# Dense products of a hybrid diffusion layer: three fp32r products of split operands, or one fp32 product

## The chip, the core and the metric

The kernel runs on one core of a Trainium2 chip. The metric is device microseconds of one execution. Five engines with queues of their own share the work: TensorE (PE: matmuls, with the weight loads shown apart as PEld), VectorE (DVE), ScalarE (ACT), GpSimd (POOL) and SyncE (SP), which issues nearly all of the DMAs here.

## What is computed

One layer of a bidirectional RWKV-7 mixer beside a gated short convolution, over 128 context tokens and 2048 latent tokens (2176 in all) of 1024 channels. Cut to the dense products:

```python
h = rmsnorm(x, norm_g) * (1 + scale) + shift        # (2176, 1024)
proj = h @ w_in                                      # 1024 -> 4096: r, k, v, g_a, b, c, u, g_b of 512 each
lw = tanh(h @ decay_down);  w = w0 + lw @ decay_up   # two directions, 64 wide
la = h @ iclr_down;         a = sigmoid(bias + la @ iclr_up)
kk = kk * rsqrt(max(sum(kk * kk, per head), 1e-24))  # 8 heads of 64
...                                                  # delta-rule scan, both directions; short convolution
bonus = sum(r * kd * bonus_rk, per head)
u = concat(ya * silu(g_a), yb * silu(g_b)) @ w_out   # 1024 -> 1024
y = rmsnorm(x + gate * u, final_g)
```

Everything is fp32 in memory.

## The kernel before

**Split products.** TensorE has a matmul in fp32r, a reduced form of fp32. The kernel gets nearly full precision from it in this way: an operand x is copied to fp32r (the high part, by ACT), and x minus that copy is the low part (by DVE or POOL). A product is then three fp32r matmuls that add up in PSUM: high by high, high by low, low by high (lines 182 to 184 for the input projection, 1503 to 1505 for the output projection). Where one operand is exact in fp32r (a matrix of ones), or where the contraction has only 64 rows, so that both parts of the data can be stacked on 128 partitions (lora-up), two matmuls do.

**Phase 1** (`phase1`) makes the input projection. The tokens are cut into six blocks `BLK` (five of 384, one of 256), taken in three thirds of two blocks. The 34 column blocks of 128 (`cb`: 16 for k, r, v, g of the recurrence, 16 for the convolution, 2 for lora-down) each need 8 slices of the contraction, so a column block on a token block is one call of `dense`, 8 slices. `make_h` normalises a block into h with both parts. `load_w` brings a column block of the weights: the first time the raw weights come from the input (512 KB, `raw_w`), are split (`high_w` on ACT, `low_w`), and both parts are stored to a scratch tensor `wsp` in HBM (1024 KB); in the second and third thirds they are loaded from there (1024 KB). `lora_down` makes the four operands of lora-up with high and low parts stacked. In each third `recurrence` goes through 8 units (4 channel groups by 2 blocks). The order of its work on PE, DVE, ACT and POOL is written out by hand: `UNIT_FIRST` for the first third, `UNIT` for the others, lists of words, each a few instructions, with the unit that it belongs to (`+-1`: the one before). Words that matter here: `k r v g` are projections, `w0 w1 a0 a1` lora-up, `bb` and `ss` sums over a head (matmuls with a block matrix of ones), `hs ls hb lb` the split of their operands, `xk yk` and the like the split of the next weights. Then `groupB` makes the convolution's part, four column blocks a group.

**Phase 2** is the chunked recurrence: products of 64- and 32-wide tiles in plain fp32 (psF, psG, psE, psX, psS and so on), with an inverse of small triangular matrices on POOL. Its first pieces run beside the last third of phase 1. Its order is a list too (`SEQ`, and `LATE` from its 13th stage on).

**Phase 3** is the output projection. Its words are woven into `LATE`: `CL/WL` load a slice of `w_out`, `CH/WH` and `CD/WD` split it, `AL cL aL` load a tile of 128 tokens of the mixed activations, `AH cH aH` and `AD cD aD` split that, and `AP P B` are the products, 512 columns each. 17 token tiles by 2 halves by 8 slices.

Two small plain fp32 products stand beside all this: the modulation rows (`mod_rows`, 32 columns of weight) and the gate row (line 636, a weight of 2 columns).

Of the kernel before, what the change touches and what calls it, by code (L numbers as in the profile page):

```python
# [6 lines left out]
F32 = mybir.dt.float32  # L7
F32R = mybir.dt.float32r
# [41 lines left out]
UNIT_FIRST = """  # L50
k al+-2 xg+-2 yg+-2 rh+-2 bb+-2 mx+-1 rc+-1 q0+-2 vs+-2 v1+-1 q1+-2 v2+-1 shv+-1 t1+-1 ov+-1 r1+-1 kk+-1
g+-1 xr+-1 yr+-1 tp+-1 kn+-1 k1 k2 kA+-1 r2+-1 a0 r s1+-1 s0+-1 shk e1+-1 shr+-1 xv+-1 kd+-1 gt+-1 ok pp+-1
c+-1 yv+-1 ta0 sq sg+-1 tv+-1 or+-1 b0+-1 ka+-1 hs a1 b1+-1 ls xk w1 w0 v ss ta1 e2+-1 yk hb+-1 t0 vm+-1
lb+-1
"""
UNIT = """
k v1+-1 vs+-2 lb+-2 mx+-1 rc+-1 s0+-1 v2+-1 w0 shv+-1 kA+-1 bb+-2 s1+-1 q0+-2 q1+-2 kk+-1 k1 a0 r1+-1 k2
pp+-1 r2+-1 ov+-1 c+-1 kn+-1 e1+-1 g+-1 ta0 shk gt+-1 kd+-1 ok shr+-1 v or+-1 e2+-1 ka+-1 b0+-1 sq b1+-1
sg+-1 al+-1 a1 hs hb+-1 t0 ls r tv+-1 rh+-1 ta1 w1 vm+-1 ss t1 tp
# [3 lines left out]
def phase1(K):  # L63
# [17 lines left out]
    ones = tp.tile([128, 128], F32, tag="pv", name="ones", bufs=1)  # L81
    nc.sync.dma_start(ones[:], A["cst"][:, 0:128])
    onr = cp.tile([128, 128], F32R, name="onr")
    V.tensor_copy(onr[:], ones[:])
    onf = cp.tile([128, 128], F32R, name="onf")
    V.tensor_scalar(onf[:], ones[:], 0.0, 1.0, ALU.mult, ALU.add)
# [30 lines left out]
    def load_up():  # L117

        raw = ta_.tile([128, 2, 2, 512], F32, tag="x", name="upraw", bufs=1)
        for h in range(2):  # L120
            nc.sync.dma_start(raw[h * 64:h * 64 + 64], A["wup"].rearrange("n (d p) c -> p n d c", d=2))
        parts = ca.tile([128, 8, 512], F32R, tag="upx", name="ups")
        hi, lo = [parts[:, i:i + 4].rearrange("p (n d) c -> p n d c", d=2) for i in (0, 4)]
        for n in range(2):
            P.copy(hi[:, n], raw[:, n])
            (V, G)[n].tensor_tensor(lo[:, n], raw[:, n], hi[:, n].bitcast(F32), ALU.subtract)
            for d in range(2):
                up[n, d] = (hi[:, n, d], lo[:, n, d])

    kept = set()  # L130
# [12 lines left out]
    def raw_w(cb):  # L143
        raw = wp.tile([128, 8, 128], F32, tag="wr", name=f"wr{cb}_{K.u()}", bufs=2)
        nc.sync.dma_start(raw[:], A["win"][cb])
        return raw

    def high_w(cb, raw):
        w = wp.tile([128, 2, 8, 128], F32R, tag="w", name=f"w{cb}_{K.u()}", bufs=4)
        P.copy(w[:, 0], raw[:])  # L150
        return w

    def low_w(cb, raw, w, eng):
        eng.tensor_tensor(w[:, 1], raw[:], w[:, 0].bitcast(F32), ALU.subtract)  # L154
        nc.sync.dma_start(S["wsp"][cb], w[:].bitcast(F32))
        kept.add(cb)

    def make_h(j, x):
        t0, n = BLK[j]
        xt, rt = x  # L160
        hh = (hr if j in (0, 3) else hl).tile([128, 2, 8, 384], F32R, tag="h", name=f"h{j}")
# [18 lines left out]
    def products(ps, w, hh, n, ks):  # L180
        for k in ks:
            T.matmul(ps[:, :n], w[:, 0, k], hh[:, 0, k, :n], start=k == 0, stop=False)  # L182
            T.matmul(ps[:, :n], w[:, 0, k], hh[:, 1, k, :n], start=False, stop=False)  # L183
            T.matmul(ps[:, :n], w[:, 1, k], hh[:, 0, k, :n], start=False, stop=k == 7)  # L184
# [29 lines left out]
    def parts_of(t_, n, nm, eng):  # L214

        hi = ta_.tile([128, 384], F32R, tag="hsh", name=f"hsh{nm}", bufs=1)
        lo = ta_.tile([128, 384], F32R, tag="hsl", name=f"hsl{nm}", bufs=1)
        P.copy(hi[:, :n], t_[:, :n])  # L218
        eng.tensor_tensor(lo[:, :n], t_[:, :n], hi[:, :n].bitcast(F32), ALU.subtract)  # L219
        return hi, lo  # L220

    def part_sum(o, t_, n, nm, eng=G):

        hi, lo = parts_of(t_, n, nm, eng)
        ps = pax.tile([128, 384], F32, tag="ax", name=f"ps{nm}")
        T.matmul(ps[:, :n], o[:], hi[:, :n], start=True, stop=False)
        T.matmul(ps[:, :n], o[:], lo[:, :n], start=False, stop=True)
        return ps

    def norm(j, xt, eng=G):  # L230
# [8 lines left out]
        ps = part_sum(onf, acc, n, f"q{j}", eng)  # L239
# [21 lines left out]
    for i, b in enumerate((0, 2, 1, 3)):  # L261
# [28 lines left out]
        if i == 0:  # L290
            xb[0] = norm(0, x0, V)
        if i == 1:
            h0 = make_h(0, xb[0])
            next(h0)
            xb[1] = norm(1, x1, V)
# [42 lines left out]
    def recurrence(t3, units, js, lws, pre, following):  # L338
# [14 lines left out]
        raws = {}  # L353
        asked, split = [], []

        def ask():
            while asked and (len(raws) < 2):
                x, cb = asked.pop(0)
                raws[x] = cb, raw_w(cb)

        def project(x, i):
# [6 lines left out]
            if u.last:  # L368
                g2 = u.g + 1
                cb = dict(k=4, r=0, v=8, g=12)[x] + g2 if g2 < 4 else dict(k=20, r=24, v=28, g=16)[x]  # L370
                if t3:
                    wts[x] = load_w(cb)
                else:
                    asked.append((x, cb))
                    ask()

        def weight(x, i, low):
            if i >= len(units) or not U[i].last or t3:
                return
            cb, raw = raws[x]  # L380
            if not low:
                wts[x] = high_w(cb, raw)
            else:
                low_w(cb, raw, wts[x], G if x in "rg" else V)
                del raws[x]
                ask()

        def word(w, i):
# [4 lines left out]
            if w[0] in "xy" and len(w) == 2:  # L393
                return weight(w[1], i, w[0] == "y")
# [31 lines left out]
            elif w in ("hs", "hb"):  # L426
                src = u.sq if w == "hs" else u.bs
                hi = one(u, "hsh" if w == "hs" else "hb", dt=F32R)
                P.copy(hi[:, :n], src[:, :n])  # L429
                setattr(u, w, hi)  # L430
            elif w in ("ls", "lb"):
                src, hi = (u.sq, u.hs) if w == "ls" else (u.bs, u.hb)
                lw_ = one(u, "hsl" if w == "ls" else "lb", dt=F32R)
                G.tensor_tensor(lw_[:, :n], src[:, :n], hi[:, :n].bitcast(F32), ALU.subtract)  # L434
                setattr(u, w, lw_)
            elif w in ("ss", "bb"):
                hi, lw_ = (u.hs, u.ls) if w == "ss" else (u.hb, u.lb)
                ps = u.ps[w] = pax.tile([128, 384], F32, tag="ax", name=f"ps{w}{g}_{j}")
                T.matmul(ps[:, :n], onr[:], hi[:, :n], start=True, stop=False)
                T.matmul(ps[:, :n], onr[:], lw_[:, :n], start=False, stop=True)  # L440
# [6 lines left out]
            elif w in ("w0", "w1", "a0", "a1"):  # L447
                which, d = "wa".index(w[0]), int(w[1])
                ps = u.ps[w] = pmm.tile([128, 384], F32, tag="mm", name=f"up{w}_{K.u()}")
                x = lws[j][which * 2 + d]  # L450
                for m, part in enumerate(up[which, d]):
                    T.matmul(ps[:, :n], part[:, g * 128:g * 128 + 128], x[:, :n], start=m == 0, stop=m == 1)
# [81 lines left out]
        seq = [(w.split("+")[0], int(w.split("+")[1]) if "+" in w else 0) for w in (UNIT if t3 else UNIT_FIRST).split()]  # L534
# [88 lines left out]
    def gate_rows():  # L623
        for b in range(2):
            pr = None
            for k2 in range(4):
                wt = wp.tile([128, 2, 512], F32, tag="wr", name=f"wgate{b}{k2}", bufs=2)
# [30 lines left out]
    def lora_down(j, wd, wi, pre):  # L658
        n = BLK[j][1]
        nm = j % 2  # L660
        lw = [ta_.tile([128, 384], F32R, tag=f"lw{i}_{nm}", name=f"lw{i}_{j}") for i in range(4)]
        for which, (w, fn) in enumerate(((wd, AF.Tanh), (wi, AF.Copy))):
            ps = pre[which] if pre else dense(w, hs[j], n, f"l{which}")
            f = ta_.tile([128, 384], F32, tag=("sq", "bs")[which], name=f"lf{which}_{j}", bufs=1)
            P.activation(f[:, :n], ps[:, :n], fn)
# [101 lines left out]
I@15 sv51@12 fa@10.1 Ge0@16 E110@13 Ev001@13 gh10@14 E010@13 Ev110@13 E100@13 gh00@14 Ev010@13 Gm1@16  # L767
# [881 lines left out]
```

## Time and profile before

| | |
|---|---|
| median of 3 runs | 1581.41 us (1579.3 to 1582.26) |
| the profiled execution, first to last instruction | 1578.3 us |
| mean granted TensorE clock | 0.982 |
| PE MATMUL records | 16208 |
| HBM read, written | 208.05 MB, 103.17 MB |

The page of the profile gives busy time by engine, the chain of work that ended last, and groups of instructions by line. A row of the timeline has the start in us, the duration in us, the engine, the line, the operation, the tiles (out<-in), the tile of the array (128\*128: contraction rows by output columns), the shape of the moving operand, and how many such instructions in a row were merged. In a group's row the numbers behind the bar are busy us and mean ns of one, then the idle time ahead of it. Matmul records overlap, since one starts before the last one's results are out; the distance between starts tells the rate.

### The profile page before, as it was taken

How to read it: one execution, taken by the hardware profiler on the slowest of the kernel's cores; microseconds unless marked ns; L12 is line 12 of the kernel's file. 1: busy time of each engine (PE TensorE's matmuls, PEld its weight loads, DVE VectorE, ACT ScalarE, POOL GpSimd, SP SyncE). 2: the span in 40 equal slices, each digit the busy share in tenths (PEclk: the TensorE clock that was granted, in tenths of full speed). 3: DMA queues.
4: the chain of work that ended last, by engine and by line, in shares of the span. 5: the costliest groups of instructions: out<-in, count | busy, mean ns of one | idle time of the engine just before them, and what ended most of it. 6: DMA issues, size and time to landing. Idle time of an engine off the chain costs nothing.

```text
span 1578.3 us, 39371 instructions
## 1 busy us (share of the span) xinstructions
PE 1499.9 (95%) x16208; PEld 1381.2 (88%) x16208; DVE 1139.9 (72%) x1957; ACT 772.3 (49%) x1462; POOL 573.8 (36%) x962
## 2 busy tenths in 40 slices
PE   5999999999999999999999998999999998899998
PEld 2899999999999999899998997888888886678786
DVE  5999995764999735449985428798998997746533
ACT  4566652432555213135551107887878777523222
POOL 0133330001333100013322805888788887212221
PEclk7899999999999999999999998999999999999999
DMA  9669998663878865438887537566676754646442
GB/s 371 213 174 264 269 270 332 223 223 115 225 220 217 233 226 180 145 116 233 261 218 267 194 125 178 150 188 159 194 192 179 193 163 149 180 142 188 151 143 93
DMA packets 204579, 313.78 MB, mean 199 GB/s; under 512 B 58088, under 2 KB 147560, under 8 KB 190320
## 3 DMA queue, kind: packets, MB, share of 16 engines
q1 hardware_dynamic: 168816, 311.13, 63.9%
q10 hardware_dynamic: 35584, 0.14, 1.4%
q8 instruction: 127, 2.08, 0.6%
q14 instruction: 52, 0.43, 0.1%
HBM read 208.05 MB, written 103.17 MB: 197 GB/s over the span
## 4 chain that ended last, share of the span: by engine, by line
PE 65%; DVE 14%; POOL 7%; issue 5%; DMA 5%; ACT 2%; SPq 0%; ACTq 0%; DVEq 0%; POOLq 0%
POOL zt L1094 4%; PE psu L1503 4%; PE psu L1504 4%; PE psu L1505 4%; PE psE L1189 3%; POOL ztmp L1091 3%; PE mmb L182 2%; PE mmb L184 2%; PE mmb L183 2%; PE psS L1220 2%; PE mmc L182 2%; PE mmc L184 2%; PE mmc L183 2%; PE mmu L182 2%; PE mmu L184 2%
## 5 line engine op out<-in xcount | busy, mean ns | idle before, releaser
L1094 POOL TENSOR_TENSOR zt<-zt,ztmp 128x30 f32<-128x30 f32 (+7 forms) x510 | 215.4, 422 | 39.8
L1091 POOL TENSOR_TENSOR ztmp<-ab,zt 128x60 f32<-128x60 f32 (+7 forms) x255 | 139.4, 547 | 66.7 <-DVE ab L1082 47.0
L410 POOL TENSOR_TENSOR sh<-rawl 128x384 f32<-128x384 f32 (+1 forms) x48 | 47.5, 1007 | 210.1 <-ACT rawl L401 210.1
L1220 PE MATMUL psS<-sv,E 128*64 128x64 f32 x2176 | 104.6, 229 | 12.8 <-DVE sv L1246 7.3
L1220 PEld LDWEIGHTS psS<-sv,E 128*64 128x64 f32 x2176 | 82.8, 137 | 37.9 <-issue 16.3
L1194 DVE TENSOR_TENSOR E<-psE,msk 128x512 f32<-128x512 f32 x136 | 90.6, 683 | 20.0 <-PE psE L1189 18.9
L1568 POOL TENSOR_TENSOR z<-z,x 128x512 f32<-128x512 f32 x32 | 42.7, 1337 | 147.6 <-DVE z L1562 85.7
L1175 ACT ACTIVATE stf<-psX 64x512 f32<-64x512 f32 x136 | 80.3, 590 | 13.1 <-PE psX L1171 10.7
L434 POOL TENSOR_TENSOR hsl<-sq,hsh 128x384 fp32r<-128x384 f32 (+1 forms) x24 | 34.1, 1421 | 129.9 <-ACT hsh L429 121.6
L1246 DVE TENSOR_TENSOR sv<-psS,pc 64x128 f32<-64x128 f32 x254 | 63.7, 271 | 22.4 <-PE psS L1220 21.7
L182 PE MATMUL mmg<-h,w 128*128 128x384 f32 (+1 forms) x216 | 70.8, 328 | 0.0
L183 PE MATMUL mmg<-h,w 128*128 128x384 f32 (+1 forms) x216 | 70.7, 327 | 0.0
L184 PE MATMUL mmg<-h,w 128*128 128x384 f32 (+1 forms) x216 | 70.7, 327 | 0.0
L219 POOL TENSOR_TENSOR hslq<-ssq,hshq 128x384 fp32r<-128x384 f32 (+1 forms) x4 | 4.8, 1202 | 174.2 <-ACT hshq L218 109.6
L182 PE MATMUL mmb<-h,w 128*128 128x384 f32 (+1 forms) x192 | 63.9, 333 | 4.0 <-DMA w<-scr_wsp 4.0
L182 PE MATMUL mmv<-h,w 128*128 128x384 f32 (+1 forms) x192 | 63.1, 329 | 0.9 <-DVE sg L524 0.6
L184 PE MATMUL mmc<-h,w 128*128 128x384 f32 (+1 forms) x192 | 62.8, 327 | 1.0 <-DVE w L154 1.0
L184 PE MATMUL mmb<-h,w 128*128 128x384 f32 (+1 forms) x192 | 63.7, 332 | 0.0
L183 PE MATMUL mmb<-h,w 128*128 128x384 f32 (+1 forms) x192 | 63.6, 331 | 0.0
L182 PE MATMUL mmu<-h,w 128*128 128x384 f32 (+1 forms) x192 | 63.0, 328 | 0.2
L182 PE MATMUL mmc<-h,w 128*128 128x384 f32 (+1 forms) x192 | 63.0, 328 | 0.0
L184 PE MATMUL mmu<-h,w 128*128 128x384 f32 (+1 forms) x192 | 62.9, 328 | 0.0
(312 smaller groups left out, 5019.6 us busy)
## 6 DMA issues: line engine op xcount, KB each, us to landing
w<-scr_wsp SPq DMA_DIRECT2D x68, 1024.0 KB, 5.4
scr_wsp<-w SPq DMA_DIRECT2D x34, 1024.0 KB, 6.0
rr<-scr_ops SPq DMA_DIRECT2D x32, 1024.0 KB, 6.7
scr_ops<-xs SPq DMA_DIRECT2D x160, 192.0 KB, 6.5
wr<-in_win SPq DMA_DIRECT2D x34, 512.0 KB, 8.2
x<-in_x SPq DMA_DIRECT2D x17, 512.0 KB, 3.9
wadas<-in_wada SPq DMA_DIRECT2D x8, 1024.0 KB, 13.9
sv<-scr_vt SPq DMA_DIRECT2D x32, 256.0 KB, 4.0
```

Source lines behind the costliest of these rows:

```text
L182: T.matmul(ps[:, :n], w[:, 0, k], hh[:, 0, k, :n], start=k == 0, stop=False)
L183: T.matmul(ps[:, :n], w[:, 0, k], hh[:, 1, k, :n], start=False, stop=False)
L184: T.matmul(ps[:, :n], w[:, 1, k], hh[:, 0, k, :n], start=False, stop=k == 7)
L1091: G.tensor_tensor(tv, ab[:, j:j + 2, j + 2:32].unsqueeze(1).broadcast_to((128, kn, 2, n)), zt[:, :kn, j:j + 2].unsqueeze(3).broadcast_to(( ...
L1094: G.tensor_tensor(zt[:, :kn, j + 2:32], zt[:, :kn, j + 2:32], tv[:, :, r], ALU.subtract)
L1175: P.activation(g.fs[64:128, :, hd, e::2], g.ps["X"][e][hr_].rearrange("p a (b t) -> p b a t", b=2), AF.Copy, scale=-1.0)
L1194: V.tensor_tensor(g.E[n][:, k:k + 2].rearrange("p a b c -> p (a b) c"), pe[:].rearrange("p a b c -> p (a b) c"), B.msk[:, ME[g.d]].unsquee ...
L1220: T.matmul(g.sp[i // 4][r, q, hd, :], g.E[n][:, k, hd, r], g.sv[:, u, hd, :], start=True, stop=True)
L1246: V.tensor_tensor(dst, g.sp[i // 4][0:64, q], B.pc[0:64, d, 2 * p:2 * p + 2, c:c + 1].broadcast_to((64, 2, 64)), ALU.mult)
L1503: T.matmul(ps[:], mh[:, n], hi[:, cs], start=start and n == 0, stop=False)
L1504: T.matmul(ps[:], mh[:, n], lo[:, cs], start=False, stop=False)
L1505: T.matmul(ps[:], ml[:, n], hi[:, cs], start=False, stop=stop and n == 3)
```

## The change

Each dense product becomes a single matmul of unsplit fp32 operands. Every split (copy to fp32r, subtraction) goes, and with them the stores of split weights and the loads of them; weights are loaded raw each time. `h`, the weights, the lora operands and the activations of the output projection need half the room, and the freed room is given to more buffers (8 of `w`, 3 each of the activations). The lora-up operands are no longer stacked: the product contracts over the 64 rows of its direction. `UNIT` loses the words of the splits, and the first third uses it as well; `LATE` loses its split words, with the others in their old order.

```diff
-UNIT_FIRST = """
...
 UNIT = """
-k v1+-1 vs+-2 lb+-2 mx+-1 ...
+k v1+-1 vs+-2 mx+-1 rc+-1 s0+-1 v2+-1 w0 shv+-1 kA+-1 bb+-2 s1+-1 q0+-2 q1+-2 kk+-1 k1 a0 r1+-1 k2 pp+-1 r2+-1 ov+-1 c+-1 kn+-1 e1+-1 g+-1 ta0 shk gt+-1 kd+-1 ok shr+-1 v or+-1 e2+-1 ka+-1 b0+-1 sq b1+-1 sg+-1 al+-1 a1 t0 r tv+-1 rh+-1 ta1 w1 vm+-1 ss t1 tp
...
-    onr = cp.tile([128, 128], F32R, name="onr")
-    V.tensor_copy(onr[:], ones[:])
+    onr = cp.tile([128, 128], F32, name="onr")
+    nc.sync.dma_start(onr[:], A["cst"][:, 0:128])
...
+        raw = ca.tile([128, 2, 512], F32, tag="upx", name="ups")
+        nc.sync.dma_start(raw[:], A["wup"].rearrange("n p c -> p n c"))
...
+                up[n, d] = raw[d * 64:d * 64 + 64, n]
...
     def load_w(cb):
-        if cb in kept:
-            w = wp.tile([128, 2, 8, 128], F32R, tag="w", name=f"w{cb}_{K.u()}", bufs=4)
-            nc.sync.dma_start(w[:].bitcast(F32), S["wsp"][cb])
-            return w
-        raw = raw_w(cb)
-        w = high_w(cb, raw)
-        low_w(cb, raw, w, V)
+        w = wp.tile([128, 8, 128], F32, tag="w", name=f"w{cb}_{K.u()}", bufs=8)
+        nc.sync.dma_start(w[:], A["win"][cb])
         return w
...
                 V.scalar_tensor_tensor(xt[:, k, c], xt[:, k, c], gs[:, k % 4, s:s + 1], rt[:, c], ALU.mult, ALU.mult)
-                P.activation(hh[:, 0, k, c], xt[:, k, c], AF.Identity, bias=sh[:, k % 4, s:s + 1])
-                V.scalar_tensor_tensor(hh[:, 1, k, c], xt[:, k, c], sh[:, k % 4, s:s + 1], hh[:, 0, k, c].bitcast(F32), ALU.add, ALU.subtract)
+                P.activation(hh[:, k, c], xt[:, k, c], AF.Identity, bias=sh[:, k % 4, s:s + 1])
...
-            T.matmul(ps[:, :n], w[:, 0, k], hh[:, 0, k, :n], start=k == 0, stop=False)
-            T.matmul(ps[:, :n], w[:, 0, k], hh[:, 1, k, :n], start=False, stop=False)
-            T.matmul(ps[:, :n], w[:, 1, k], hh[:, 0, k, :n], start=False, stop=k == 7)
+            T.matmul(ps[:, :n], w[:, k], hh[:, k, :n], start=k == 0, stop=k == 7)
...
-                T.matmul(ps[:, :n], onr[:], hi[:, :n], start=True, stop=False)
-                T.matmul(ps[:, :n], onr[:], lw_[:, :n], start=False, stop=True)
+                T.matmul(ps[:, :n], onr[:], src[:, :n], start=True, stop=True)
...
-                x = lws[j][which * 2 + d]
-                for m, part in enumerate(up[which, d]):
-                    T.matmul(ps[:, :n], part[:, g * 128:g * 128 + 128], x[:, :n], start=m == 0, stop=m == 1)
+                T.matmul(ps[:, :n], up[which, d][:, g * 128:g * 128 + 128], lws[j][which][d * 64:d * 64 + 64, :n], start=True, stop=True)
...
-            for d in range(2):
-                a, b = slice(d * 64, d * 64 + 64), slice(64 - d * 64, 128 - d * 64)
-                t_ = lw[which * 2 + d]
-                V.tensor_copy(t_[a, :n], f[a, :n])
-                V.tensor_tensor(t_[b, :n], f[a, :n], t_[a, :n].bitcast(F32), ALU.subtract)
+            P.activation(lw[which][:, :n], ps[:, :n], fn)
...
     def w_load(k):
-        raws["w", k] = O.r.tile([128, 1024], F32, tag="raw", name=f"woraw{k}", bufs=2)
-        D(raws["w", k][:], A["wout"][k * 128:(k + 1) * 128, :])
...
         if k in ATT:
+            wk[k] = K.spare((8, 4, 0, 2)[k], f"wo{k}", F32)
+        D(wk[k][:], A["wout"][k * 128:(k + 1) * 128, :])
...
+            mx = mts[a, i] = (O.r if a == "c" else O.l).tile([128, 4, 128], F32, tag=f"m{a}", name=f"m{a}{i}", bufs=3)
...
-            T.matmul(ps[:], mh[:, n], hi[:, cs], start=start and n == 0, stop=False)
-            T.matmul(ps[:], mh[:, n], lo[:, cs], start=False, stop=False)
-            T.matmul(ps[:], ml[:, n], hi[:, cs], start=False, stop=stop and n == 3)
+            T.matmul(ps[:], ms[:, n], wk[k][:, cs], start=start and n == 0, stop=stop and n == 3)
```

More of the change, by code (lines that the diff above doesn't have):

```diff
@@ L80, in phase1 @@
     nc.sync.dma_start(vec[:], A["vec"])
-    ones = tp.tile([128, 128], F32, tag="pv", name="ones", bufs=1)
-    nc.sync.dma_start(ones[:], A["cst"][:, 0:128])
-    onr = cp.tile([128, 128], F32R, name="onr")
-    V.tensor_copy(onr[:], ones[:])
-    onf = cp.tile([128, 128], F32R, name="onf")
-    V.tensor_scalar(onf[:], ones[:], 0.0, 1.0, ALU.mult, ALU.add)
+    onr = cp.tile([128, 128], F32, name="onr")
+    nc.sync.dma_start(onr[:], A["cst"][:, 0:128])
+    onf = cp.tile([128, 128], F32, name="onf")
+    V.memset(onf[:], 1.0)
     smask = ca.tile([128, 384], F32, name="smask")
@@ L160, in make_h @@
         xt, rt = x
-        hh = (hr if j in (0, 3) else hl).tile([128, 2, 8, 384], F32R, tag="h", name=f"h{j}")
+        hh = (hr if j in (0, 3) else hl).tile([128, 8, 384], F32, tag="h", name=f"h{j}")
         hs[j] = hh
@@ L212, in mod_rows, with norm @@
             T.matmul(ps[q:q + 32, :], scp[:, k, :], wt[:, i, :], start=k < 4, stop=k >= 4)
[L214 to L230, printed above, removed]
+    def norm(j, xt):
         t0, n = BLK[j]
@@ L238, in norm @@
             V.tensor_tensor(acc[:, :n], acc[:, :n], sq[:, :n], ALU.add)
-        ps = part_sum(onf, acc, n, f"q{j}", eng)
+        ps = pax.tile([128, 384], F32, tag="ax", name=f"psq{j}")
+        T.matmul(ps[:, :n], onf[:], acc[:, :n], start=True, stop=True)
         rt = ta_.tile([128, 384], F32, tag="kk", name=f"rt{j}", bufs=1)
@@ L290, in phase1 @@
         if i == 0:
-            xb[0] = norm(0, x0, V)
+            xb[0] = norm(0, x0)
         if i == 1:
@@ L294, in phase1 @@
             next(h0)
-            xb[1] = norm(1, x1, V)
+            xb[1] = norm(1, x1)
             first_products(wlora, range(4))
@@ L352, in recurrence @@
             U.append(u)
[L353 to L359, printed above, removed]
         def project(x, i):
@@ L370, in project @@
                 cb = dict(k=4, r=0, v=8, g=12)[x] + g2 if g2 < 4 else dict(k=20, r=24, v=28, g=16)[x]
[L371 to L386, printed above, removed]
+                wts[x] = load_w(cb)
         def word(w, i):
@@ L532, in word @@
                 spill("q", g, j, u.q, "q")
-        seq = [(w.split("+")[0], int(w.split("+")[1]) if "+" in w else 0) for w in (UNIT if t3 else UNIT_FIRST).split()]
+        seq = [(w.split("+")[0], int(w.split("+")[1]) if "+" in w else 0) for w in UNIT.split()]
         E = mybir.EngineType
@@ L626, in gate_rows @@
             for k2 in range(4):
[L627 removed]
+                wt = wp.tile([128, 2, 512], F32, tag="w", name=f"wgate{b}{k2}", bufs=8)
                 nc.sync.dma_start(wt[:], A["wada"][4 + b][:, k2 * 2:k2 * 2 + 2])
@@ L660, in lora_down @@
         nm = j % 2
-        lw = [ta_.tile([128, 384], F32R, tag=f"lw{i}_{nm}", name=f"lw{i}_{j}") for i in range(4)]
+        lw = [ta_.tile([128, 384], F32, tag=f"lw{i}_{nm}", name=f"lw{i}_{j}") for i in range(2)]
         for which, (w, fn) in enumerate(((wd, AF.Tanh), (wi, AF.Copy))):
             ps = pre[which] if pre else dense(w, hs[j], n, f"l{which}")
-            f = ta_.tile([128, 384], F32, tag=("sq", "bs")[which], name=f"lf{which}_{j}", bufs=1)
-            P.activation(f[:, :n], ps[:, :n], fn)
-            for d in range(2):
-                a, b = slice(d * 64, d * 64 + 64), slice(64 - d * 64, 128 - d * 64)
-                t_ = lw[which * 2 + d]
-                V.tensor_copy(t_[a, :n], f[a, :n])
-                V.tensor_tensor(t_[b, :n], f[a, :n], t_[a, :n].bitcast(F32), ALU.subtract)
+            P.activation(lw[which][:, :n], ps[:, :n], fn)
         return lw
@@ L1596, in end @@
             p.close()
[L1598 to L1600 removed]
+    K.last = dict(R=lambda _=0: begin(), Lo=lambda _=0: begin_left(), end=end, CL=w_load, WL=w_load,
+                  AL=m_load("c"), cL=m_load("c"), aL=m_load("a"), xL=x_load, ss=square_sum, rt=root, rc=inverse_root, fo=out)
     for h in range(2):
@@ L1625, in build @@
             K.S[name] = tc.dram_tile(list(shape), F32, name=f"scr_{name}")[:]
-    K.S["wsp"] = tc.dram_tile([34, 128, 2, 8, 128], F32, name="scr_wsp")[:]
     phase3(K)
```

154 lines of the change are left out of this document (41 added, 113 removed).

## The prediction, made before the change was run

> **What bounds the kernel now.** I read the page's busy shares and its chain first, then the stage table (busy time of each engine in stretches that I chose, with the number of instructions, the granted TensorE clock and the DMA share), then single records of PE.
>
> ```profile
> PE 1499.9 (95%) x16208; PEld 1381.2 (88%) x16208; DVE 1139.9 (72%) x1957; ACT 772.3 (49%) x1462; POOL 573.8 (36%) x962
> ...
> PE 65%; DVE 14%; POOL 7%; issue 5%; DMA 5%; ACT 2%; SPq 0%; ACTq 0%; DVEq 0%; POOLq 0%
> ```
>
> ```profile
> core 0: us, PE busy (x) PEld busy (x) DVE busy (x) ACT busy (x) POOL busy (x), PEclk, DMA share, GB/s
> 0.00:60.00 60.00, 39.42 (x190) 25.87 (x191) 40.91 (x99) 28.77 (x55) 2.04 (x16) 0.77 0.87 325
> 60.00:240.00 180.00, 174.63 (x998) 171.10 (x998) 170.39 (x213) 108.73 (x194) 65.11 (x49) 1.00 0.86 240
> 240.00:800.00 560.00, 559.34 (x3330) 548.27 (x3329) 387.62 (x607) 225.34 (x411) 89.38 (x77) 1.00 0.68 210
> 800.00:840.00 40.00, 35.89 (x220) 34.93 (x219) 29.93 (x52) 13.21 (x29) 6.75 (x7) 0.91 0.80 224
> 840.00:960.00 120.00, 115.42 (x1137) 111.44 (x1138) 57.77 (x116) 24.14 (x55) 42.18 (x91) 0.97 0.56 189
> 960.00:1300.00 340.00, 320.57 (x8204) 283.40 (x8202) 300.46 (x606) 267.81 (x508) 286.32 (x616) 0.99 0.65 178
> 1300.00:1371.00 71.00, 57.06 (x1214) 48.53 (x1206) 51.60 (x100) 50.37 (x86) 39.21 (x74) 0.95 0.50 151
> 1371.00:1570.00 199.00, 196.90 (x945) 157.40 (x941) 98.04 (x164) 52.93 (x128) 42.81 (x33) 1.00 0.47 152
> ```
>
> PE's busy time can't be read as work done, because records overlap (a 384-column matmul shows 0.33 us, but the next one starts 0.17 us later). What counts is the distance from start to start. The stretches that hold the dense products are 60 to 960 (input projection) and 1371 to 1570 (output projection): PE is idle there for 5.4, 0.7, 4.1, 4.6 and 2.1 us. So in nearly all of the time that the change touches, TensorE is the bound, at full clock, and whatever a product costs more or less goes into the time one to one. The middle, 960 to 1300, holds the recurrence, which the change leaves alone. DVE comes near PE in one place, 60 to 240, with 170.4 of 180 us; the change takes work away from it there.
>
> **What a dense product costs now.** In the order of time on PE, the first and the last of 24 matmuls of one block (8 slices of the contraction, three fp32r matmuls each):
>
> ```profile
> 560.67 0.34 PE L182 MATMUL mmc<-h,w 128*128 128x384 f32 x1
> ...
> 564.66 0.34 PE L184 MATMUL mmc<-h,w 128*128 128x384 f32 x1
> ```
>
> 23 steps in 3.99 us are 0.1735 us each, so one slice of 384 columns costs 3 x 0.1735 = 0.5205 us. The same reading for 256 columns (17 steps in 2.04 us) and for the 512 of the output projection (18 steps in 4.09 us):
>
> ```profile
> 940.89 0.28 PE L182 MATMUL mmgb<-h,w 128*128 128x256 f32 x1
> ...
> 942.93 0.28 PE L184 MATMUL mmgb<-h,w 128*128 128x256 f32 x1
> ```
>
> ```profile
> 1372.74 0.40 PE L1505 MATMUL psa<-woh,mlc 128*128 128x512 f32 x1
> ...
> 1376.83 0.39 PE L1505 MATMUL psa<-woh,mlc 128*128 128x512 f32 x1
> ```
>
> These give 0.120 and 0.227 us, 0.360 and 0.682 a slice.
>
> **What a plain fp32 product costs.** No plain fp32 product of full size is in the trace. The nearest is the gate row (L636): a [128 x 2] weight with 512 moving columns, amid the dense stream.
>
> ```profile
> L636 PE MATMUL psgate<-gaterow,sel x4: 590/591/592, 600.8 to 653.7; 128*2 128x512 f32 x4
> ```
>
> ```profile
> 600.54 0.34 PE L183 MATMUL mmc<-h,w 128*128 128x384 f32 x1
> 600.81 1.02 PE L636 MATMUL psgate<-gaterow,sel 128*2 128x512 f32 x2
> 601.76 0.44 PE L226 MATMUL psq<-hshq,onf 128*128 128x384 f32 x1
> ```
>
> The loop makes two such products and the trace shows four records: **an fp32 product is two matmuls on the chip**. Entering it took 0.27 us where a 384 step takes 0.1735, so a change of the tile in the array (128\*128 to 128\*2) costs 0.0965 us. Leaving it costs that again, and the rest, 0.95 - 0.0965 = 0.853 us, is two records of 0.427 us for 512 columns, 0.834 ns a column each. For 384 columns that is 0.641 us a product, for 256 0.427, for 512 0.854. The width of the weight was 2 here and will be 128; whether the wider load hides is told by the fp32 loads of 128 columns, which take 0.141 us, less than half of a 0.32 us pass:
>
> ```profile
> L1317 PEld LDWEIGHTS psT<-idt,y x68: 137/141/144, 1057.6 to 1490.6; 128*128 128x128 f32 x68
> ```
>
> Bounds: from below, two records could run side by side, as the 64-wide ones of the recurrence do (16 records of 128 columns in 1348.85 - 1347.83 - 0.0965 = 0.92 us, half of 16 x 0.107); then a 384 product costs 0.32 us. From above, four steps like today's, 4 x 0.1735 = 0.694 us.
>
> ```profile
> 1347.83 1.09 PE L1189 MATMUL psE<-stg,stf 128*64 128x128 f32 x16 [1.20 <-DVE E L1194]
> 1348.85 0.66 PE L1317 MATMUL psT<-idt,y 128*128 128x128 f32 x4
> ```
>
> I take 0.641, because the gate row is the only row with a long moving operand and no neighbour in the other columns of the array; the side-by-side rows all use two or more column halves, and a 128-wide weight has none to spare. The Trainium skill (FP8 and Floating Point Precision, TensorE Precision Notes) counts four passes for true fp32; the row agrees, 0.853 us being four times 0.213. With today's step for each pass the sum would be that of the second rival.
>
> **The sum, part by part.**
>
> - Input projection and lora-down: 34 column blocks x 8 slices x 5 token blocks of 384 = 1360 products, x (0.641 - 0.5205) = +163.9 us; 272 of 256 columns x (0.427 - 0.360) = +18.2.
> - Output projection: 17 token tiles x 2 halves x 8 = 272 of 512 columns x (0.854 - 0.682) = +46.8.
> - Lora-up and sums by ones (bb, ss, and the norm's) were two fp32r matmuls and become one fp32 product:
>
> ```profile
> L452 PE MATMUL upa<-lw,ups x96: 279/337/418, 69.5 to 807.5; 128*128 128x384 f32 x80, 128*128 128x256 f32 x16
> ...
> L452 PE MATMUL upw<-lw,ups x96: 278/338/443, 70.2 to 811.3; 128*128 128x384 f32 x80, 128*128 128x256 f32 x16
> ```
>
> ```profile
> L439 PE MATMUL psbb<-hb,onr 128*128 128x384 f32 x20 | 6.8, 342 | 0.0
> L439 PE MATMUL psss<-hsh,onr 128*128 128x384 f32 x20 | 6.7, 337 | 0.0
> ...
> L226 PE MATMUL psq<-hshq,onf 128*128 128x384 f32 x5 | 2.2, 450 | 0.0
> ```
>
>   Half of the 192 records are 96 up products: 80 x (0.641 - 0.347) + 16 x (0.427 - 0.240) = +26.5. Sums: 45 x 0.294 + 9 x 0.187 = +14.9.
> - Up products now contract over 64 rows, not 128, a tile of another shape amid full ones (k, **w0**, bb, **a0**, g, v, **a1**, r, tv, **w1**, ss in UNIT). Two changes each: 96 x 2 x 0.0965 = +18.5 us; from nothing (if rows alone don't count) to this, and I take it, since every change of shape in the rows above pays it.
>
> Together +288.8 us on PE, none of it beside other PE work.
>
> **What goes away.** The splits leave ACT, DVE and POOL, the stores of split weights (34 of 1024 KB) leave the DMA queues, and reloads shrink from 1024 to 512 KB. All of that lies beside a busy PE, so it is worth only the PE idle time that it ends. The rows of the chain where it stood on the path:
>
> ```profile
> 21.91 0.95 DVE w L154
> ...
> 25.61 1.08 DVE w L154
> ...
> 45.43 1.15 DVE w L154
> ```
>
> ```profile
> 1363.20 1.05 ACT woh L1473
> 1364.33 2.39 POOL wol L1477
> 1366.73 3.46 DMA mxc<-scr_mixT
> ```
>
> By stage: start-up 4 us (three splits of 3.2 us and a shorter make_h; the 14 us of loading ahead of it stays); 60 to 240, 998 records at 0.1735 are 173 of 180 us, 7 saved; 240 to 800, 1; 800 to 840, 6 (4.1 idle, and a clock of 0.91 is 3.6 us more); 1300 to 1371, 4 of 13.9 idle (the split before the first output product; the rest waits for the recurrence's own E and X); 1371 on, 4. Sum -26, between -12 and -45. Nothing late takes its place: what the removed work hid behind PE, PE still hides, and DVE only gets freer. The deeper buffers (w 8, m 3 of each) add no wait that I can find: a weight column block has the products of two token blocks, 2 x 8 x 0.641 = 10 us, in which the next one of 512 KB can land, and SP's loads of m stand a tile (14 us) ahead of use.
>
> Net +263 us: 1578.3 + 263 = 1841 us of span. The median of the runs is 1581.41, 3.1 over this span, so **1844 us**, 17% slower.
>
> **The rivals.**
>
> 1. *The other side: the two records of a product overlap.* Then 384 columns cost 0.32 us: -272.7 - 39.8 - 69.4 - 2.5 - 1.4 + 18.5 = -367 us on PE, of which DVE would give back some 50 (60 to 240 can't fall much under 150 us with DVE at 170.4 now): about 1265 us. The kernel isn't slower if a 384 product costs under 0.512 us, records 0.256 us apart. For it: the paired records of psE. Against it: the gate row, whose two records follow each other. The Trainium skill (Perfetto Trace Analysis, Engine Utilization) halves the array's output rate for FP32_LOW_HIGH; read as the rate of a whole product that is this rival, while the trace shows that rate for one record, and two are needed. Chance 0.03.
> 2. *Every pass keeps the overhead of today's.* A step of 0.1735 us is 0.0135 more than 384 columns at 0.417 ns. Four full steps a product: +236 + 32.6 + 61.9 + 31.6 + 17.8 + 18.5 - 26 = +372, 1953 us. With the overhead once a record (2 x 0.0135 x 2054 products = +55) it is 1899. Against it: 0.853 us in the gate row is 4 x 512 x 0.4166 ns with nothing over. Chance 0.05 for the first; the second is in the range.
> 3. *More is won back than I see*, under 1806 us: the start-up's 20.6 idle us and the 13.9 before the output projection would have to go as well, though loads and the recurrence end them. Chance 0.04.
>
> **How the numbers follow.** Forecast 0.88. Low end: no price for the 64-row tiles, 45 us won back: 1844 - 18.5 - 19 = 1806. High end: 0.0135 on each record and a little less won back: 1905. Differences under 0.2% can't be told from none here. Faster is the first rival, 0.03; within 0.2% would need the break-even 0.512 us by chance, 0.01; slower 0.96.
>
> **What would show it.** In the changed kernel: dense records of 384 columns 0.32 us apart, two a slice (0.1735 and three before; over 0.333 speaks for rival 2, under 0.2 for rival 1); the stretch of the first third without idle PE and with DVE well under 90%; about 0.1 us lost on entering and on leaving each up product; no scr_wsp among the DMA issues; the recurrence's middle 340 us as long as now. I would be wrong if the weight's width counts in an fp32 pass, which no row here shows, or if the granted clock falls.

## The result, and the profile after

The changed kernel takes **1869.99 us** (median of 4 runs, 1868.24 to 1871.92), the kernel before in the same measurement 1581.84 (4 runs, 1579.3 to 1582.82). The ratio is 1.183, 95% interval 1.180 to 1.186: 288 us slower, where +263 was forecast. The profiled execution after has a span of 1869.8 us.

The page of the changed kernel, busy shares, traffic, chain and the issue that loads the weights:

```profile
PE 1805.8 (97%) x14304; PEld 1140.8 (61%) x14304; DVE 992.1 (53%) x1785; ACT 692.7 (37%) x1330; POOL 458.8 (25%) x897
...
HBM read 171.88 MB, written 67.52 MB: 128 GB/s over the span
...
PE 80%; POOL 13%; issue 2%; DVE 2%; DMA 1%; ACT 0%; SPq 0%; DVEq 0%; POOLq 0%; ACTq 0%
...
w<-in_win SPq DMA_DIRECT2D x102, 512.0 KB, 3.6
```

Everything that the change was to take away went: 36 MB less read and 36 MB less written, DVE 1140 to 992 us, POOL 574 to 459, and no store of split weights is left among the issues. PE has 1900 records fewer and is busy for 306 us more.

The stage table, cut where the thirds of the first phase, the entry to the recurrence, the recurrence and the output projection begin. First the changed kernel (columns as in the prediction's table), then the kernel before:

```profile
core 0: us, PE busy (x) PEld busy (x) DVE busy (x) ACT busy (x) POOL busy (x), PEclk, DMA share, GB/s
...
60.00:437.00 377.00, 377.00 (x1151) 212.04 (x1150) 183.92 (x304) 114.69 (x211) 18.59 (x24) 1.00 0.39 106
437.00:842.00 405.00, 405.00 (x1248) 223.68 (x1247) 184.33 (x281) 111.37 (x196) 20.67 (x24) 1.00 0.38 109
842.00:1186.00 344.00, 344.00 (x1476) 230.08 (x1475) 161.91 (x269) 86.99 (x174) 60.55 (x115) 1.00 0.36 108
...
1203.00:1260.00 57.00, 50.31 (x1082) 44.58 (x1075) 34.21 (x69) 34.87 (x67) 37.28 (x87) 0.85 0.48 131
1260.00:1620.00 360.00, 332.99 (x8239) 292.46 (x8240) 309.14 (x632) 272.61 (x513) 278.42 (x596) 0.98 0.64 177
1620.00:1869.00 249.00, 242.45 (x668) 107.50 (x666) 75.68 (x134) 35.35 (x97) 40.39 (x32) 0.99 0.37 121
```

```profile
61.00:356.00 295.00, 289.63 (x1662) 286.10 (x1661) 243.25 (x358) 149.06 (x257) 67.60 (x51) 1.00 0.80 246
356.00:671.00 315.00, 314.48 (x1796) 304.08 (x1795) 211.03 (x313) 118.74 (x214) 52.28 (x42) 1.00 0.66 195
671.00:946.00 275.00, 270.75 (x2016) 266.30 (x2016) 177.38 (x286) 90.85 (x190) 82.43 (x130) 0.99 0.66 202
...
963.00:1008.00 45.00, 42.22 (x1101) 37.18 (x1096) 33.37 (x67) 34.46 (x65) 38.41 (x85) 0.99 0.56 159
1008.00:1371.00 363.00, 332.42 (x8248) 291.85 (x8242) 315.89 (x634) 281.30 (x524) 286.60 (x603) 0.99 0.63 174
1371.00:1578.00 207.00, 197.59 (x947) 157.62 (x942) 101.16 (x170) 53.95 (x131) 42.81 (x33) 0.99 0.46 149
```

The three thirds grow by 82, 90 and 69 us, the output projection by some 43, the first two stages of the recurrence (entry) by 12; the rest of the recurrence is 3 shorter. In the first phase of the changed kernel PE isn't idle for a hundredth of a microsecond, with DVE at 46 to 49% of each third and the DMA engines at 0.36 to 0.39. The entry is the one surprise: its granted clock is 0.85, where it was 0.99.

What a product costs, from blocks that follow each other on PE in the changed kernel (16 records are the 8 products of a block):

```profile
1162.39 5.32 PE L144 MATMUL mmgb<-h,w 128*128 128x384 f32 x16
1167.55 5.32 PE L144 MATMUL mmb<-h,w 128*128 128x384 f32 x16
1172.71 3.62 PE L144 MATMUL mmc<-h,w 128*128 128x256 f32 x16
1176.17 3.62 PE L144 MATMUL mmu<-h,w 128*128 128x256 f32 x16
```

```profile
1707.31 3.60 PE L1373 MATMUL psu<-wo,mc 128*128 128x512 f32 x8
...
1721.04 3.60 PE L1373 MATMUL psu<-wo,mc 128*128 128x512 f32 x8
```

From start to start: 5.16 us for 16 records are **0.3225 us a record** of 384 columns, two of them a product of 0.645; 3.46 / 16 = 0.216 for 256; 13.73 us for the 32 records between the two psu rows are 0.429 for 512. So a slice of the contraction costs 0.645 us where three fp32r products cost 0.5205, 1.24 times as much.

### The profile page after: what moved, and what is told of

Same layout as the page of the kernel before. It is cut to its first block, busy times and chain, and to the rows that moved or that the text cites. A ratio compares the mean times of both kernels' runs of the same rounds, so it can differ in the third digit from the quotient of the medians.

```text
span 1869.8 us, 35065 instructions
## 1 busy us (share of the span) xinstructions
PE 1805.8 (97%) x14304; PEld 1140.8 (61%) x14304; DVE 992.1 (53%) x1785; ACT 692.7 (37%) x1330; POOL 458.8 (25%) x897
## 4 chain that ended last, share of the span: by engine, by line
PE 80%; POOL 13%; issue 2%; DVE 2%; DMA 1%; ACT 0%; SPq 0%; DVEq 0%; POOLq 0%; ACTq 0%
PE psu L1373 12%; POOL zt L987 8%; PE mmg L144 7%; PE mmc L144 6%; PE mmb L144 6%; PE mmv L144 6%; PE mmu L144 6%; PE mmr L144 6%; PE mmk L144 6%; PE mmgb L144 5%; POOL ztmp L984 5%; PE mml L144 3%; PE psE L1082 2%; PE upw L359 2%; PE upa L359 2%
## 5 line engine op out<-in xcount | busy, mean ns | idle before, releaser
L144 PE MATMUL mmg<-h,w 128*128 128x384 f32 (+1 forms) x432 | 138.6, 475 | 0.0
L1373 PE MATMUL psu<-wo,ma 128*128 128x512 f32 x272 | 122.1, 594 | 0.0
L144 PE MATMUL mmr<-h,w 128*128 128x384 f32 (+1 forms) x368 | 118.0, 474 | 0.0
L144 PE MATMUL mmk<-h,w 128*128 128x384 f32 (+1 forms) x368 | 115.6, 467 | 0.0
L144 PEld LDWEIGHTS mmg<-h,w 128*128 128x128 f32 x432 | 80.3, 190 | 56.1 <-ACT pp L373 8.2
L144 PE MATMUL mmgb<-h,w 128*128 128x384 f32 (+1 forms) x336 | 105.9, 467 | 0.0
L1373 PE MATMUL psu<-wo,mc 128*128 128x512 f32 x224 | 101.3, 595 | 0.0
L144 PEld LDWEIGHTS mmv<-h,w 128*128 128x128 f32 x384 | 72.7, 190 | 45.1 <-ACT q L325 1.1
L144 PEld LDWEIGHTS mmu<-h,w 128*128 128x128 f32 x384 | 73.0, 190 | 44.1
L144 PEld LDWEIGHTS mmb<-h,w 128*128 128x128 f32 x384 | 72.6, 190 | 43.9 <-issue 0.7
```

What stands on the lines that cost most here:

```text
L144: T.matmul(ps[:, :n], w[:, k], hh[:, k, :n], start=k == 0, stop=k == 7)
L1373: T.matmul(ps[:], ms[:, n], wk[k][:, cs], start=start and n == 0, stop=stop and n == 3)
```

## The experiments

**The changed kernel again**, for the scatter, and as the base of the three variants measured beside it: the up products over 128 rows, the split output projection and the preset copies on POOL.

> The changed kernel itself, a second trace of it. Theory A (the recurrence's entry is late by its order: 12 copies of preset tiles on DVE ahead of the first transposes, PE idle for 4 us, half clock after it): again about 1203 us from the start to the first psX and 417 us from there to the first output product, against 408.5 in the kernel before; total 1870. Theory B (the extra 8 us of the recurrence is scatter from execution to execution): the second stretch differs by several us from 417, towards 408, and the total with it.

1872.11 us (1870.55 to 1877.01), ratio 1.178 (1.173 to 1.183). The first phase has the same three lengths to a tenth, 376.5, 405.5 and 344.0 us from the first lora-down product of one third to that of the next, the last up to its last block of dense products. The recurrence, from its first psX product to psa, the first of the output projection, took 413.7 us against 416.6. Where PE is the bound the trace repeats itself to 0.1 us; the recurrence scatters by 3.

**The up products over 128 rows.** Each up weight lies in a tile of its own with zeros in the other direction's 64 rows, and the product takes all 128 rows of the lora operand, so that no 64-row tile is left.

```diff
-        raw = ca.tile([128, 2, 512], F32, tag="upx", name="ups")
+        raw = ca.tile([128, 4, 512], F32, tag="upx", name="ups")
+        G.memset(raw[:], 0.0)
...
-                up[n, d] = raw[d * 64:d * 64 + 64, n]
+                nc.sync.dma_start(raw[d * 64:d * 64 + 64, n * 2 + d], A["wup"][n, d * 64:d * 64 + 64])
+                up[n, d] = raw[:, n * 2 + d]
...
-                T.matmul(ps[:, :n], up[which, d][:, g * 128:g * 128 + 128], lws[j][which][d * 64:d * 64 + 64, :n], start=True, stop=True)
+                T.matmul(ps[:, :n], up[which, d][:, g * 128:g * 128 + 128], lws[j][which][:, :n], start=True, stop=True)
```

> The changed kernel with lora-up over all 128 rows: the weights of each direction stand on their 64 partitions, zeros on the other 64, so the tile of the array is 128*128 like its neighbours'. Theory A (each entry into and exit from the 64-row tile costs 0.093 us): 96 products x 2 x 0.093 = 17.9 us less, 1852 us. Rival (the tile's change is hidden, or the time of a product goes by its rows): no change, 1870, or more.

1838.85 us (1835.35 to 1841.82), ratio 1.157 (1.152 to 1.163): 33 us under the changed kernel of the same measurement, where 17.9 were expected. The thirds are 365.5, 393.8 and 332.3 us, 11.0, 11.7 and 11.7 less: **34.4 us for 178 changes of shape, 0.19 us each**, twice the price taken. (Two for each of the 96 up products would be 192; in the changed kernel's trace seven pairs of them already stand next to each other, six of these in the first two units of a third, where no bb lies between w0 and a0.) The rows of PE around a pair of up products show where it sits, first in the changed kernel, then in this one:

```profile
560.72 0.91 PE L359 MATMUL upw<-lw,ups 64*128 64x384 f32 x2
561.56 0.91 PE L349 MATMUL psbb<-bs,onr 128*128 128x384 f32 x2
562.40 0.91 PE L359 MATMUL upa<-lw,ups 64*128 64x384 f32 x2
563.24 5.43 PE L144 MATMUL mmg<-h,w 128*128 128x384 f32 x16
568.50 5.32 PE L144 MATMUL mmv<-h,w 128*128 128x384 f32 x16
```

```profile
547.35 0.81 PE L360 MATMUL upw<-lw,ups 128*128 128x384 f32 x2
547.99 0.81 PE L350 MATMUL psbb<-bs,onr 128*128 128x384 f32 x2
548.64 0.81 PE L360 MATMUL upa<-lw,ups 128*128 128x384 f32 x2
549.28 5.32 PE L145 MATMUL mmg<-h,w 128*128 128x384 f32 x16
```

Between starts stand 0.84 us where they are 0.64 to 0.65 without the change of shape: each product here has a change at both ends. psbb, of full shape itself, pays as much as the up products beside it. The block mmg behind them lasts 5.43 instead of 5.32 us, so a change costs on both of its sides: some 0.09 us ahead of it, and 0.10 on the first record after. Single records of the trace say the same: they start 0.416 and 0.426 us apart on the two sides of the change at 560.72, where 0.3225 is the rule.

**The up products in pairs.** The same products in another order: w0 a0 and a1 w1 stand next to each other, so 96 of the 178 changes of shape are left.

```diff
-v2+-1 w0 shv+-1 kA+-1 bb+-2
+v2+-1 w0 a0 shv+-1 kA+-1 bb+-2
...
-k1 a0 r1+-1
+k1 r1+-1
...
-a1 t0 r tv+-1 rh+-1 ta1 w1 vm+-1
+a1 w1 t0 r tv+-1 rh+-1 ta1 vm+-1
```

> The changed kernel with its 64-row up products two by two on PE (w0 a0, and a1 w1, next to each other in UNIT), so that 192 changes of the tile's shape become 96; the same products otherwise. Theory (each change of shape costs 0.18 us, half of it on the record before and half on the first record after): -17 us, 1853, 5.7 us less in each third (370.8, 399.8, 338.3). Rival (the price sits in the product of 64 rows itself, 0.36 us each wherever it stands): 1870, thirds as they were (376.5, 405.5, 344.0).

1850.87 us (1848.94 to 1859.91), ratio 1.165 (1.161 to 1.169); the changed kernel's two ratios were 1.183 and 1.178; 1853 us were expected. The thirds are 371.4, 400.1 and 338.6 us: 5.1, 5.4 and 5.4 less, 15.9 for the 82 changes that go, 0.19 each. It's the change of shape that costs, not the product of 64 rows:

```profile
555.34 0.91 PE L359 MATMUL upw<-lw,ups 64*128 64x384 f32 x2
556.09 0.81 PE L359 MATMUL upa<-lw,ups 64*128 64x384 f32 x2
556.82 0.91 PE L349 MATMUL psbb<-bs,onr 128*128 128x384 f32 x2
557.57 5.32 PE L144 MATMUL mmg<-h,w 128*128 128x384 f32 x16
```

A change at one end only gives 0.73 to 0.75 us, and the mmg block, now behind a product of its own shape, is back at 5.32. The Trainium skill (TensorEngine Tiling (Array Packing), Key Properties) says that a change of the tiling mode, though not of the tile alone, drains the array; the runs agree that a change of shape costs time and put a price to it, but that a drain is what takes it they don't show.

**The changed kernel with the split output projection of before** (its LATE list, `w_load`, `w_high`, `w_low`, `m_high`, `m_low` and the three fp32r products a slice), **and the reverse**, the kernel before with only its output projection in fp32.

```diff
-            T.matmul(ps[:], ms[:, n], wk[k][:, cs], start=start and n == 0, stop=stop and n == 3)
+            hi, lo = wk[k]
+            T.matmul(ps[:], mh[:, n], hi[:, cs], start=start and n == 0, stop=False)
+            T.matmul(ps[:], mh[:, n], lo[:, cs], start=False, stop=False)
+            T.matmul(ps[:], ml[:, n], hi[:, cs], start=False, stop=stop and n == 3)
```

> The changed phase 1 with the output projection of the kernel before (three fp32r products and their splits). By the records, 272 products of 512 columns cost 0.176 us less each, 47.9, and the splits bring back 4 to 5 us of waits: 43 us less than the changed kernel, 1827. Rival (the recurrence's extra 8 us come from the changed order of the output words in the late list): 8 us less still, 1819, and 408 us from the first psX to the first output product. By theory A that stretch stays near 417 or longer by the splits.

> The kernel before up to the end of the recurrence, with the output projection of the changed kernel (single fp32 products, no splits of wo and m). Theory (the cost sits in the PE time of the products, and the recurrence's extra 8 us of the changed kernel come from its changed first phase): +43 us, all of it after the first output product (207 -> 250), 1581.8 + 43 = 1625; the stretch from the first psX to the first psa stays at 408 +-2 us, with 23 and 22 us for its first two stages. Rival (the extra 8 us come from the changed list of the output's steps, or are scatter from execution to execution): the stretch is 413 to 418 here too, 1630 to 1635.

Split again: 1832.36 us (1827.27 to 1834.19), ratio 1.152 (1.147 to 1.157), 40 under the changed kernel where 43 were expected. fp32 alone in the kernel before: 1625.81 (1624.03 to 1631.18) against 1585.63, ratio 1.025 (1.023 to 1.028), 40 over, again with 43 expected. The end stretch from the first psa on is 208.2 and 250.3 us, so the term lies where it was put and is the same in either company. The stretch of the recurrence told the rest: 417.8 us, of which its first two stages took 53.7, with the first phase of the changed kernel and the old list; 409.2 and 46.8 with the first phase of before and the new list. The list of the output's steps isn't what lengthens the entry.

**One term alone: the sums by ones** as fp32 products in the kernel before, without the splits of their operands.

```diff
-                hi, lw_ = (u.hs, u.ls) if w == "ss" else (u.hb, u.lb)
+                src = u.sq if w == "ss" else u.bs
...
-                T.matmul(ps[:, :n], onr[:], hi[:, :n], start=True, stop=False)
-                T.matmul(ps[:, :n], onr[:], lw_[:, :n], start=False, stop=True)
+                T.matmul(ps[:, :n], onr[:], src[:, :n], start=True, stop=True)
```

> The kernel before with only the sums by ones (bb, ss and the norm's) as single fp32 products, without the splits of their operands. Theory: 45 products of 384 columns cost 0.646 instead of 0.347 us, 9 of 256 cost 0.432 instead of 0.240: +15 us on PE, 1 to 2 of it won back from the splits, 1595 us. Rival (the splits that go, on ACT and POOL, free more than they show, or the sums lie off the bound): within 4 us of 1582.

1595.49 us (1592.93 to 1602.09) against 1585.63, ratio 1.0065 (1.0041 to 1.009): +10 us, interval 6.5 to 14.3. The sign and most of the 13 to 14 expected are there; the scatter of the kernel before, which was 10 us in this measurement, allows no finer reading. In the trace the thirds are 298.4, 322.5 and 275.3 us, against 295.0, 314.8 and 275.5 before: the last third shows none of its share of some 4 us, so this run bears out the sign and the size, but not the place.

**How far down PE is the bound.** Two cuts in PE's work in the first phase: the kernel before without the third fp32r product of a slice in the input projection and lora-down, and the changed kernel with 4 of the 8 slices there.

```diff
-            T.matmul(ps[:, :n], w[:, 0, k], hh[:, 1, k, :n], start=False, stop=False)
-            T.matmul(ps[:, :n], w[:, 1, k], hh[:, 0, k, :n], start=False, stop=k == 7)
+            T.matmul(ps[:, :n], w[:, 0, k], hh[:, 1, k, :n], start=False, stop=k == 7)
```

```diff
-            T.matmul(ps[:, :n], w[:, k], hh[:, k, :n], start=k == 0, stop=k == 7)
+            if k < 4:
+                T.matmul(ps[:, :n], w[:, k], hh[:, k, :n], start=k == 0, stop=k == 3)
```

> The kernel before without the third fp32r product of a slice in the input projection and lora-down (the low part of the weight by the high part of h is left out of the result); the splits and stores stay. Theory (PE is the bound, one to one, with DVE and DMA close behind in the first third only): PE has 1360 x 0.1735 + 272 x 0.12 = 269 us less; the first third, where DVE is at 170 and the DMA engines at 0.86 of 180 us, gives back 28 to 50: 1341 to 1363 us. Rival (DVE or the loads bind soon after PE gets faster in all of phase 1): over 1400 us.

> The changed kernel with only the first 4 of the 8 slices of each product of the input projection and lora-down (the other half of the contraction is left out of the result), so that a column block costs PE what it would if the two records of a product ran side by side. Theory (PE is the bound far down, since DVE has 530 and the DMA engines 0.38 of 1126 us in the first phase of the changed kernel): 1360 x 0.323 + 272 x 0.216 = 498 us less, and 0 to 30 of it given back: 1372 to 1400. Rival (as with two of three products, where 111 of 269 us came out: DVE, ACT and the waits between units bind soon after PE): about 41% of 498 comes out, 1665.

The kernel before came to 1474.25 us (1470.5 to 1476.42; ratio 0.929, 0.927 to 0.931): 111 of the 269 us, and the expectation of 1341 to 1363 missed by far. The changed kernel came to 1420.89 (1418.02 to 1421.76; ratio to the kernel before 0.894, 0.891 to 0.896): 449 of the 498 us, 21 over the upper end expected. The stage table over the whole first phase, of the one and of the other:

```profile
55.00:832.00 777.00, 672.59 (x3901) 633.11 (x3900) 634.00 (x967) 361.44 (x671) 195.30 (x223) 0.93 0.84 246
```

```profile
60.00:733.00 673.00, 645.20 (x2205) 362.01 (x2204) 522.83 (x849) 306.76 (x578) 84.78 (x118) 0.99 0.66 177
```

With the splits in place PE has 104 idle us in the phase, the DMA engines are at 0.84, and the granted clock falls to 0.93. Without them PE is idle for 28, at 0.99. So the kernel before stood close to its other limits, and the change did take those away; the room it makes is worth nothing while PE has more to do than before. Of the 158 us that didn't come out in the two-of-three kernel, 94 are idle time of PE that wasn't there before (104 against 10), and some 50 go with the lower clock (0.07 x 777 = 54, against 3 before). By the trace's waits nearly all of that idle time ends with ACT (some 60 us) or DVE (some 32), and 5 with a load; which of them would bind alone no run separates.

**The entry to the recurrence.** In the changed kernel PE's longest wait at the entry is for DVE's zr, behind the presets that DVE copies; here POOL makes those copies.

```profile
1190.35 1.42 DVE L809 COPY sth<-I 64x512 f32<-64x512 f32 x4
1191.68 1.03 DVE L995 STREAM_TRANSPOSE zr<-zt 128x512 f32<-128x512 f32 x1
```

```diff
-            V.tensor_copy(t_[0:64, 0, hd], B.I2[0:64].unsqueeze(1).broadcast_to((64, 8, 64)))
+            G.tensor_copy(t_[0:64, 0, hd], B.I2[0:64].unsqueeze(1).broadcast_to((64, 8, 64)))
```

> The changed kernel with the recurrence's preset copies (identity blocks into the stf, stg and sth tiles, 12 copies of 0.36 us on DVE at the entry) on POOL, which is idle there. Theory A: PE's wait of 4.2 us on the first transpose falls to under 1.5, less half clock follows, and the time falls by 4 to 10 us, 1860 to 1866. Theory B (scatter) or a later bound at the entry (its loads land at the same time): within 2 us of 1870.

> The kernel before once more, for a second trace of its recurrence. If the changed first phase makes the recurrence longer, the stretch from first psX to first psa is 408 +-2 us again, its first two stages 23 and 22 us. If the 8 us are scatter between executions, it lies anywhere between 408 and 418.

1876.43 us (1871.23 to 1877.38), ratio 1.180 (1.175 to 1.185): nothing gained, where 4 to 10 us were expected. PE's waits from the last dense products to the recurrence's third stage, in the changed kernel and then in this one (who waits and for whom, us in total, times, the longest; issue means that the profile shows nothing that PE waited for):

```profile
PE psU L1012 <- DVE zr L995: 4.2, 1, 4.2
PE psX L1064 <- issue: 3.3, 1, 3.3
PE psGm L912 <- issue: 2.6, 1, 2.6
```

```profile
PE psGm L912 <- issue: 3.7, 1, 3.7
PE psW L1020 <- ACT zd L1015: 3.6, 1, 3.6
PE psX L1064 <- issue: 2.0, 1, 2.0
...
PE psU L1012 <- DVE zr L995: 0.6, 1, 0.6
```

The wait for zr fell from 4.2 to 0.6 us, and a wait for ACT's zd of 3.6 took its place; its two first stages took 60 us. The second trace of before (one execution, 1590.26 us) has its two first stages in 45 us again (23.0 and 21.9), but its recurrence took 412.9 us, not 408.4. Over all traces with the first phase of before the two stages took 45 to 48 us, with that of the changed kernel 50 to 60; the whole stretch took 408 to 413 and 409 to 418. The low end of the last is the kernel with the up products in pairs (408.9; the one with half a contraction took 409.0). So some of the 8 us is scatter, and some of it sits in the entry. The entry of the kernel with the up products in pairs, in its stage table:

```profile
1191.00:1241.00 50.00, 45.98 (x1081) 40.95 (x1078) 33.03 (x66) 33.92 (x64) 35.53 (x82) 0.90 0.50 136
```

Its two stages took 50 us at a clock of 0.90. Multiplied by the granted clock they are 45 us here, 45 before (45 x 0.99) and 48 in the changed kernel (57 x 0.85). By this arithmetic some 8 of the 12 us go with the lower clock, and the waits marked issue are about the rest. The changed kernel's trace shows the order of the two:

```profile
1203.00:1209.50 6.50, 3.21 (x84) 2.61 (x79) 0.79 (x3) 3.63 (x8) 5.48 (x14) 1.00 1.06 346
1209.50:1219.80 10.30, 10.30 (x132) 8.91 (x129) 3.67 (x7) 7.70 (x14) 8.89 (x19) 0.50 0.06 19
1219.80:1240.20 20.40, 18.32 (x496) 16.23 (x492) 15.71 (x32) 12.22 (x25) 9.83 (x27) 1.00 0.62 170
1240.20:1247.10 6.90, 6.28 (x78) 5.95 (x80) 2.85 (x6) 3.25 (x6) 5.96 (x13) 0.51 0.01 3
```

The clock is at a half in two stretches. The two waits marked issue end at 1208.5 and 1240.8, so each of the two stretches begins after its wait had begun, and the waits come first here. In the kernel with the presets on POOL the clock falls at 1197.5 already, ahead of the wait for zd that ends at 1202.5, with waits of 0.6 and 1.3 us before it. No run is without such waits; so that they cause the low clock isn't shown, and what sets the waits stays open.

## Why the prediction held, point by point

- **PE is the bound, one to one:** held. The three thirds show no idle PE at all, and the two experiments on the output projection moved the time by 40 us each, where the records give 272 x (0.858 - 0.682) = 48 and the splits that go give a few back.
- **An fp32 product is two records of 0.834 ns a column:** held, 0.3225, 0.216 and 0.429 us a record at 384, 256 and 512 columns, for a weight of 128 columns as for one of 2. The forecast was 2 to 2.5 ns a record short (0.3225 against 0.3205); over some 2050 products of two records that is 8 to 9 us. "With nothing over", which rival 2 was weighed by, came from taking 0.0965 us off the gate row's 0.95 for leaving it, as much as entering had cost; two records of 0.429 leave 0.092 for that. The Trainium skill (TensorE: Matmul & The Clock Gate, Back-to-back issue gap) has columns / 2.4 GHz + 2.5 ns between matmuls at full clock; the three sizes agree, if a record of fp32 is counted as twice its columns.
- **Changes of shape, 96 x 2 x 0.0965 = 18.5 us:** the right mechanism, half its size. It measures 34.4, for 178 changes instead of 192, 0.19 each. The step priced a change by how much later the next record *started*, 0.27 for 0.1735 us, and not by what that record then paid itself. The fence it was read from had the second half: the psq row behind the gate row lasts 0.44 us, the dense records around it 0.34.
- **Won back, 26 us:** the sum was nearly right and its places were not. By the measured records the additions come to 169.3 + 19.6 (input projection) + 47.9 (output) + 26.9 (up) + 15.1 (sums) + 34.4 (shapes) = 313 us; the trace grew by 291.5, so 22 came back. Some 4.6 us of the additions lie in the start-up, which was 0.9 us shorter in this trace; it gave back 5.5 here, but 2 to 4 in the traces where it ended later (4 forecast). The first phase had 260.7 us of additions and grew by 240.7, so it gave back 20, not 14: its 10 us of idle PE, and more that its busy figures hid. The output gave 5 (4 forecast). The recurrence with its entry took 8 instead of giving 4.
- **From 1844 to 1870:** +8.5 for the records, +16 for the shapes, +4 less won back, and -3 because the changed kernel's runs lie 0.2 us over its span, not 3.1.
- **The rivals:** the first (two records side by side, 1265 us) needs records under 0.256 us apart at 384 columns, and they are 0.3225. The changed kernel with half a contraction, a cut of that kind, gave back 49 of 498 us, as much as the rival's allowance of 50; but that was set for DVE in the first third, and PE's waits there are for ACT more than for DVE, so the match of the two is luck. The second needs 0.347 a record, or 0.334 with the overhead once; neither is there. The third needed more than 45 us won back, and 22 were.
- **What would show it:** records 0.32 us apart, no idle PE in the first third with DVE under 50%, no scr_wsp, and a recurrence past its entry of 360 against 363 us all came true. The 0.1 us on entering and leaving an up product came out at 0.19 for each change. The clock, named as what could make it wrong, did fall, but in the entry alone.

## What to carry to other kernels

Price a change of number format by the distance from start to start at the sizes used, and count the records of a product: here one fp32 product takes 0.645 us and the three fp32r products that it replaces 0.5205, so splits that run beside a busy TensorE are cheaper than the 0.1245 us a slice that it costs to go without them. When a product of another row count is put amid full ones, count its two changes of shape, and both sides of each; put such products next to each other or pad them to the full shape. Freed engines and traffic are worth only the idle time of the bound that they end: 72 MB less traffic and 148 us less of DVE bought some 22 us here.

## What the runs showed that I had not expected

- A change of the array's tile shape costs 0.19 us here, half of it on the far side, and a full-size product between two 64-row ones pays it as well (0.84 instead of 0.645 us).
- Padding a contraction of 64 rows with zeros to 128 made the changed kernel 33 us faster: the rows that are left empty cost nothing, the change of shape does.
- The kernel before and the changed one are both bound by PE, but with very different room behind it: 41% of the PE time cut from the one came out in the time, 90% of that cut from the other.
- In the two-of-three kernel, where PE waits more often, its granted clock over the first phase was 0.93, where the kernel before had 0.99 to 1.00 in each third: PE's waits there came with slower products.
